# A bidirectional hybrid trunk on one core: the instruction order from a timeline simulation

## The chip, the cores and the metric

The kernel runs on one of the eight cores of a Trainium2 chip. The metric is device time in microseconds (us) from the program's start to its end; lower is better. A core has five engines, each with a queue of its own that is worked off in order: TensorE (PE; its weight loads are listed as PEld), VectorE (DVE), ScalarE (ACT), GpSimd (POOL) and SyncE (SP, which here only issues DMAs). An instruction that waits for another engine holds up all that stand behind it in its queue, so the order of each queue is part of the program.

## The reference

One inference step over 384 tokens (128 of a prompt, 256 of a latent sample), width 1024, two layers. A conditioning vector gives shift, scale and gate of every sub-layer (`mod`).

```python
mod = silu(cond) @ w_mod[l] + b_mod[l]          # 6 * 1024 values per layer
shift1, scale1, gate1, shift2, scale2, gate2 = jnp.split(mod, 6, axis=-1)
m, st = mix_fn(rmsnorm(x, g[0]) * (1 + scale1) + shift1)
x = x + gate1 * rmsnorm(m, g[1])
f = jnp.square(jax.nn.relu((rmsnorm(x, g[2]) * (1 + scale2) + shift2) @ w_up)) @ w_down
x = x + gate2 * rmsnorm(f, g[3])
```

In layer 0 the mixer has an SSD (Mamba-2) and an RWKV-7 head group, in layer 1 a GLA and an mLSTM group, all of them in both directions:

```python
# RWKV-7, per head and token
s = s * exp(lw_t) - (s @ kk_t) * (kk_t * a_t) + v_t * k_t
# mLSTM, per head and token
h = num / jnp.maximum(jnp.abs(den), jnp.exp(-m_t))
```

## The kernel before

**Dense products.** Each projection is made of `dps` products on TensorE: activations and weights are split into a high and a low part, and three products are added (high by high, low by high, high by low). A weight panel `raw` is loaded by SP (line 689), its high part `wH` copied by ACT (L277), its low part `wL` taken by DVE (L235). These products wait for little and can stand almost anywhere.

**Layer 0 mixer (AB).** The recurrence of RWKV is worked in 16 steps (8 pairs of heads, 2 directions). In each a triangular matrix is inverted by five doublings. One doubling is the product `pz`, two copies `Zb` on ACT, the products `pw` and `pt`, and two subtractions on DVE that give the next `W` and `T`:

```python
pz = pairs("pz", self.AOb[n % 2], Tm)
for h in halves:
    self.acopy(Zb[h, :, h], zv[h])
pw = pairs("pw2", Zb, W)
self.tt(f(W2), f(W), pw, ALU.subtract)
self.tt(f(T2), f(Tm), pt[:, :T], ALU.subtract)
```

The products `pe`, then `pc`, end an inversion and feed the chain `pr`, `pu`, `pd`, `py` over four segments. The tiles of the inversion exist once, so the 16 inversions run one after the other. Beside them stand the SSD core (`aux`), the dense products of the input projection and of the output projection (its last panel is `wlast`), and the modulations of later sub-layers.

**Modulations.** For each of eight slices k of the conditioning, four products write four column quarters of one accumulator. The weights come from a pool of 20 tiles:

```python
for g, w in enumerate(raw.pop(0)):
    self.mm(a[32 * g:32 * g + 32], self.cond[:, k, :], w, start=k == 0, stop=k == KD - 1)
```

In the MLP of layer 0 the generator of this block is advanced once and then behind three panels of the down projection (`if j in (2, 4, 6): next(mod)`), and the rest is left for the turn to the layer 1 mixer.

**Layer 1 mixer (CD).** Four heads of GLA and four of mLSTM, with dense products between. An mLSTM head ends with the products `ps<-mv,mE` and `ps<-CN,mq`, the sum `num` and its normalisation on DVE (`den`, `mo`), a norm over the head (`hsq` on ACT, `hss` on DVE), and six transposes `ps<-const_base,mo` on TensorE. A GLA head ends with the same transposes of `go`.

**What sets the order.** The program is written as generators that are interleaved by step counts and a table of paces (`run`, line 1578). From this text a list scheduler makes each engine's queue: it keeps a simulated time for each engine, and of the instructions that are ready at that time it takes the first one in program order. What is ready when, and so the order, follows from the durations that its simulation gives. The choice of buffers in the pools follows too.

## Time and profile before

| | us |
|---|---|
| median of 3 runs | 1856.34 (1852.14 to 1859.11) |
| the profiled execution | 1855.77 |
| its span, first to last instruction | 1853.7 |
| TensorE busy in the span | 1763.3 |
| granted TensorE clock, mean | 0.98 |

The stages in the profile: opening 0 to 125 us, AB 125 to 790, output projection and the turn to the MLP 790 to 870, the MLP of layer 0 to 1145, the turn to CD to 1200, CD to 1545, the turn to 1600, the MLP of layer 1 to the end. In the views a line such as L221 is a line of the kernel, a name such as `dps<-sH,wH` is the tile written and the tiles read. TensorE's float32 products of a `mod` appear as two records each.

### The profile page before, as it was taken

Reading aid. Unit: us, or ns where it says so; the run is one execution under the profiler, and the core shown is the slowest. Engines: PE = TensorE matmul, PEld = TensorE weight load, DVE = VectorE, ACT = ScalarE, POOL = GpSimd, SP = SyncE. Lnnn points to the kernel's source line nnn. Section 1 sums busy time; section 2 is a strip of 40 time slices with the busy share of each in tenths; the row PEclk is TensorE's granted clock in tenths of the full one; section 3 lists DMA queues with packets and bytes.
Section 4 is the critical chain, followed back from the end, with each engine's and each line's share of the span. In section 5 each row is a group of like instructions: output and inputs, shape, how many; then the busy total and the mean of one; then the engine's idle time right before and its main releaser. Section 6 shows DMA issues by size and latency. Waiting matters only on the chain.

```text
span 1853.7 us, 37402 instructions
## 1 busy us (share of the span) xinstructions
PE 1763.3 (95%) x13667; PEld 1479.4 (80%) x13667; DVE 1302.7 (70%) x2992; ACT 1068.7 (58%) x2688; POOL 216.8 (12%) x270
## 2 busy tenths in 40 slices
PE   7879999999999999999999999899999998999998
PEld 3677767666666777786999997889989897999887
DVE  3698788777877888768765335686786958766434
ACT  3567475747564776646654332676676756755322
POOL 3222111120112011111000000020211212000000
PEclk9889999999999999999999999999999998999999
DMA  8332443333334322345445544333333233344432
GB/s 280 114 87 75 122 136 87 106 93 112 100 103 125 99 60 86 100 129 161 126 125 176 164 143 107 84 98 103 101 94 92 74 109 106 115 125 126 149 135 80
DMA packets 314107, 213.55 MB, mean 115 GB/s; under 512 B 39648, under 2 KB 297494, under 8 KB 313924
## 3 DMA queue, kind: packets, MB, share of 16 engines
q1 hardware_dynamic: 308756, 208.35, 38.5%
q10 hardware_dynamic: 4816, 2.69, 0.5%
q8 instruction: 107, 1.75, 0.4%
q14 instruction: 76, 0.62, 0.1%
q0 software_dynamic: 352, 0.13, 0.0%
HBM read 201.32 MB, written 9.78 MB: 114 GB/s over the span
## 4 chain that ended last, share of the span: by engine, by line
PE 76%; DVE 10%; ACT 8%; issue 3%; DMA 2%; POOL 1%; SPq 1%; DVEq 0%; ACTq 0%; POOLq 0%
PE dps L221 46%; PE o L221 7%; PE ps L221 5%; PE mod L221 3%; PE aux L221 2%; DVE wL L235 2%; PE psc L221 2%; PE py L221 1%; PE pt L221 1%; PE pr L221 1%; DVE cacc L242 1%; ACT wH L277 1%; ACT Zb L277 1%; PE pw L221 1%; PE ms L221 1%
## 5 line engine op out<-in xcount | busy, mean ns | idle before, releaser
L277 ACT ACTIVATE wH<-raw 128x256 fp32r<-128x256 f32 (+1 forms) x790 | 363.2, 480 | 430.1 <-PE dps L221 305.3
L235 DVE TENSOR_TENSOR wL<-raw,wH 128x256 fp32r<-128x256 f32 (+2 forms) x771 | 399.5, 537 | 246.3 <-ACT wH L277 242.8
L277 ACT ACTIVATE Zb<-pz 64x384 f16<-64x384 f32 x160 | 77.2, 482 | 36.2 <-PE pz L221 33.8
L242 DVE SCALAR_TENSOR_TENSOR cacc<-rows,params,cacc 128x384 f32<-128x384 f32 (+1 forms) x192 | 94.2, 491 | 0.7
L221 PE MATMUL dps<-sH,wH 128*128 128x384 f32 x232 | 85.3, 369 | 5.5 <-DVE m L235 4.9
L221 PE MATMUL dps<-sL,wH 128*128 128x384 f32 x232 | 80.0, 345 | 0.3 <-DVE sL L235 0.2
L221 PE MATMUL dps<-sH,wL 128*128 128x384 f32 x232 | 79.4, 343 | 0.5 <-DVE wL L235 0.5
L221 PE MATMUL dps<-h0H,wH 128*128 128x384 f32 (+1 forms) x147 | 59.5, 406 | 11.9 <-ACT h0H L277 7.3
L235 DVE TENSOR_TENSOR AO<-AHb,rwmask 128x768 f16<-128x768 f16 (+1 forms) x112 | 60.0, 537 | 7.4 <-PE pz L221 5.7
L235 POOL TENSOR_TENSOR BK<-BK,kkk 128x768 f32<-128x768 f32 x16 | 33.8, 2110 | 222.3 <-DVE BK L239 151.3
L221 PE MATMUL mod<-xT,cond 128*32 128x384 f32 (+1 forms) x320 | 56.2, 490 | 3.7 <-DVE Q L235 2.5
L221 PE MATMUL dps<-h6H,wH 128*128 128x384 f32 (+2 forms) x147 | 54.8, 373 | 2.7 <-ACT wH L277 2.7
L221 PE MATMUL dps<-h4H,wH 128*128 128x384 f32 (+1 forms) x147 | 54.4, 375 | 2.1 <-ACT h4H L245 2.1
L221 PE MATMUL dps<-h2H,wH 128*128 128x384 f32 (+1 forms) x147 | 54.8, 374 | 0.0
L235 POOL TENSOR_TENSOR gDb<-gb 128x384 f32<-128x384 f32 x28 | 33.2, 1187 | 172.4 <-DVE gb L2224 73.2
L221 PE MATMUL dps<-h6H,wL 128*128 128x384 f32 (+2 forms) x147 | 50.8, 346 | 1.4 <-DVE wL L235 1.4
L221 PE MATMUL dps<-h0H,wL 128*128 128x384 f32 (+1 forms) x147 | 51.9, 353 | 0.0
L221 PE MATMUL dps<-h1H,wH 128*128 128x384 f32 (+1 forms) x147 | 51.8, 352 | 0.0
L221 PEld LDWEIGHTS dps<-sH,wH 128*128 128x128 f32 x232 | 43.6, 189 | 10.1 <-issue 5.6
L221 PE MATMUL dps<-h0L,wH 128*128 128x384 f32 (+1 forms) x147 | 51.5, 356 | 0.0
L221 PE MATMUL dps<-h1H,wL 128*128 128x384 f32 (+1 forms) x147 | 51.0, 347 | 0.0
L221 PE MATMUL dps<-h1L,wH 128*128 128x384 f32 (+1 forms) x147 | 51.0, 353 | 0.0
(1163 smaller groups left out, 5455.1 us busy)
## 6 DMA issues: line engine op xcount, KB each, us to landing
raw<-in_w_mlp_up SPq DMA_DIRECT2D x64, 512.0 KB
raw<-in_w_mlp_down SPq DMA_DIRECT2D x64, 512.0 KB
raw<-in_w_in_ab SPq DMA_DIRECT2D x204, 128.0 KB
xT<-in_w_mod SPq DMA_DIRECT2D x128, 192.0 KB
raw<-in_w_in_cd SPq DMA_DIRECT2D x192, 128.0 KB
raw<-in_w_mod SPq DMA_DIRECT2D x64, 192.0 KB
raw<-in_w_mod SPq DMA_DIRECT2D x32, 256.0 KB
raw<-in_w_out_cd SPq DMA_DIRECT2D x64, 128.0 KB
```

The lines of the kernel that those rows point to most:

```text
L221: self.nc.tensor.matmul(out, lhsT, rhs, start=start, stop=stop)
L235: (eng or self.nc.vector).tensor_tensor(out=out, in0=a, in1=b, op=op)
L242: self.nc.vector.scalar_tensor_tensor(out=out, in0=a, scalar=s, in1=b, op0=op0, op1=op1)
L277: self.nc.scalar.activation(out=out, in_=in_, func=AF.Copy)
```

## The change

The scheduler's simulation of durations is switched from its default to the timeline simulation, for the whole program:

```diff
-    with tile.TileContext(nc) as tc:
+    with tile.TileContext(nc, schedule_with_timeline_sim=True) as tc:
         build(tc, I, O)
```

The instructions, their engines and their operands stay the same; the order in each queue and the buffers change. Three places on TensorE's queue follow, each first of before, then of the change.

The MLP of layer 0, TensorE, at the modulations of layer 1 (`mod`), among the down projection (`dps<-f...`). Before:

```order
L221 MATMUL dps<-f31H,wH 128x384
L221 MATMUL dps<-f31L,wH 128x384
L221 MATMUL dps<-f31H,wL 128x384
L221 MATMUL mod<-raw,cond 32x384 x4
L221 MATMUL dps<-f0H,wH 128x384
L221 MATMUL dps<-f0L,wH 128x384
```

The change:

```order
L221 MATMUL dps<-f15H,wL 128x384
L221 MATMUL dps<-f16H,wH 128x384
L221 MATMUL dps<-f16L,wH 128x384
L221 MATMUL mod<-raw,cond 32x384
L221 MATMUL dps<-f16H,wL 128x384
L221 MATMUL dps<-f17H,wH 128x384
L221 MATMUL dps<-f17L,wH 128x384
```

Before, the 32 products stand in three groups of four in this MLP and twenty at the turn to CD; in the change 21 stand alone, two blocks have six and two, all among the down projection, and three stand at the turn.

CD, TensorE, the end of the last mLSTM head (`mo`). Before, with 54 `dps` rows between the last `ps<-CN,mq` and this piece:

```order
L221 MATMUL dps<-sH,wH 128x384
L221 MATMUL dps<-sL,wH 128x384
L221 MATMUL dps<-sH,wL 128x384
L232 MATMUL ps<-const_base,mo 128x128 x3
L221 MATMUL dps<-sH,wH 128x384
L221 MATMUL dps<-sL,wH 128x384
L221 MATMUL dps<-sH,wL 128x384
```

The change:

```order
L221 MATMUL dps<-sH,wL 128x384
L221 MATMUL ps<-mv,mE 128x257 x3
L221 MATMUL ps<-CN,mq 128x257
L221 MATMUL ps<-mv,mE 128x257
L221 MATMUL ps<-CN,mq 128x257
L232 MATMUL ps<-const_base,mo 128x128 x6
L221 MATMUL dps<-sH,wH 128x384 x2
```

The six transposes moved up to stand right behind the products that their input comes from.

AB, TensorE, the same doubling of the twelfth inversion (from its last `pz` to its first `pw`). Before:

```order
L221 MATMUL pz<-T,AO_793 128x64
L221 MATMUL pu<-R,WF 64x64 x2
L221 MATMUL dps<-h2H,wH 128x384
L221 MATMUL dps<-h2L,wH 128x384
L221 MATMUL dps<-h2H,wL 128x384
L221 MATMUL dps<-h3H,wH 128x384
L221 MATMUL dps<-h3L,wH 128x384
L221 MATMUL dps<-h3H,wL 128x384
L232 MATMUL aux<-const_base,X 128x128
L232 MATMUL aux<-const_base,Y 128x128
L221 LDWEIGHTS Zb
L221 MATMUL pw_10449<-W,Zb 128x64
```

The change:

```order
L221 MATMUL pz<-T,AO_793 128x64
L221 MATMUL pu<-R,WF 64x64 x2
L221 MATMUL py<-Q,UV 64x64
L221 LDWEIGHTS Zb
L221 MATMUL pw_10449<-W,Zb 128x64
```

The dense products that stood between have moved to earlier steps. Over the steps the number of `dps` products is, before and in the change: before the first `pe` 356 and 403; then 30, 94, 92, 52, 72, 96, 68, 52, 72, 96, 68, 60, 44, 140, 61 and 125, 120, 96, 66, 75, 123, 0, 72, 120, 60, 3, 0, 129, 36, 170; in the last step, up to the first `dps<-sH,wlast`, 155 and 10.

## Rows read from the trace of the kernel before

**Rows 1.** The page: busy times, and the chain that ended last, by line.

```profile
PE 1763.3 (95%) x13667; PEld 1479.4 (80%) x13667; DVE 1302.7 (70%) x2992; ACT 1068.7 (58%) x2688; POOL 216.8 (12%) x270
...
PE dps L221 46%; PE o L221 7%; PE ps L221 5%; PE mod L221 3%; PE aux L221 2%; DVE wL L235 2%; PE psc L221 2%; PE py L221 1%; PE pt L221 1%; PE pr L221 1%; DVE cacc L242 1%; ACT wH L277 1%; ACT Zb L277 1%; PE pw L221 1%; PE ms L221 1%
```

**Rows 2.** Windows by stage: busy time and records of each engine.

```profile
core 0: us, PE busy (x) PEld busy (x) DVE busy (x) ACT busy (x) POOL busy (x), PEclk, DMA share, GB/s
...
125.00:790.00 665.00, 641.36 (x7212) 466.55 (x7212) 541.78 (x1344) 421.09 (x1071) 98.27 (x105) 0.99 0.35 100
...
870.00:1145.00 275.00, 273.30 (x1562) 269.64 (x1561) 147.84 (x290) 126.83 (x266) 7.92 (x14) 1.00 0.47 139
1145.00:1200.00 55.00, 45.81 (x272) 37.16 (x271) 39.55 (x101) 29.91 (x78) 1.53 (x8) 0.94 0.32 76
1200.00:1545.00 345.00, 332.89 (x2047) 312.85 (x2047) 263.76 (x601) 242.76 (x706) 51.06 (x66) 0.99 0.36 100
```

**Rows 3.** The chain that ended last, in the first MLP: start, us, what.

```profile
1093.63 33.48 PE dps L221 x192
```

**Rows 4.** TensorE's timeline there: start, duration, line, operation, records.

```profile
1092.51 0.33 PE L221 MATMUL dps<-f31H,wL 128*128 128x384 f32 x1
1092.77 0.85 PE L221 MATMUL mod<-raw,cond 128*32 128x384 f32 x8
1093.56 0.44 PE L221 MATMUL dps<-f0H,wH 128*128 128x384 f32 x1
1093.83 0.34 PE L221 MATMUL dps<-f0L,wH 128*128 128x384 f32 x1
```

**Rows 5.** TensorE's timeline in AB, a single `mod` product.

```profile
198.59 0.83 PE L221 MATMUL mod<-xT,cond 128*32 128x384 f32 x2
199.35 0.45 PE L221 MATMUL dps<-h3H,wL 128*128 128x384 f32 x1
```

**Rows 6.** TensorE's timeline at the turn to CD; in brackets idle time, and what ended it.

```profile
1148.85 3.43 PE L221 MATMUL mod<-raw,cond 128*32 128x384 f32 x40
...
1152.22 3.49 PE L221 MATMUL warm<-nh,const_base 128*128 128x384 f32 x10
...
1163.32 0.58 PE L221 MATMUL dps<-h0H,wH 128*64 128x384 f32 x1 [7.33 <-ACT h0H L277]
```

**Rows 7.** TensorE's waits in CD: total, times, longest.

```profile
PE ps L232 <- DVE mo L239: 6.3, 3, 2.9
```

**Rows 8.** TensorE's timeline at the end of the last mLSTM head.

```profile
1530.01 0.60 PE L221 MATMUL ps<-CN,mq 128*128 128x257 f32 x2
...
1539.80 0.49 PE L232 MATMUL ps<-const_base,mo 128*128 128x128 f32 x3
```

**Rows 9.** Windows behind the wait of rows 6.

```profile
1163.30:1167.00 3.70, 3.68 (x12) 3.50 (x13) 3.14 (x6) 3.64 (x9) 0.00 (x0) 0.50 0.00 0
1167.00:1171.00 4.00, 4.00 (x24) 3.62 (x23) 3.44 (x9) 4.00 (x12) 0.52 (x2) 1.00 0.00 0
```

**Rows 10.** Windows of inversion steps 5, 11, 12, and the last stretch of AB.

```profile
360.50:424.10 63.60, 60.46 (x613) 42.58 (x612) 48.94 (x117) 30.76 (x89) 12.18 (x12) 0.95 0.33 95
...
645.30:680.60 35.30, 34.90 (x459) 26.95 (x458) 31.99 (x83) 23.16 (x58) 7.74 (x7) 1.00 0.25 64
680.60:712.90 32.30, 30.70 (x378) 22.61 (x378) 27.14 (x65) 28.63 (x71) 2.69 (x3) 1.00 0.20 58
...
799.80:844.40 44.60, 42.58 (x336) 34.11 (x335) 25.40 (x68) 18.63 (x48) 2.08 (x3) 1.00 0.53 161
```

**Rows 11.** TensorE's timeline in step 12: start, first doubling, and the shortest one.

```profile
680.62 0.34 PE L221 MATMUL pe<-T,i128h 128*128 128x384 f16 x1
...
690.68 0.35 PE L221 MATMUL pz<-T,AO 128*128 128x64 f16 x6
...
706.57 0.34 PE L221 MATMUL pz<-T,AO 128*128 128x64 f16 x6
707.99 0.35 PE L221 MATMUL pw<-W,Zb 128*128 128x64 f16 x6 [0.41 <-ACT Zb L277]
708.27 0.38 PE L221 MATMUL pt<-Zb,W 64*64 64x64 f16 x12
709.62 0.35 PE L221 MATMUL pz<-T,AO 128*128 128x64 f16 x6
```

## The prediction

> **What bounds the kernel now.** I read the page first: TensorE is busy for 95% of the span, and the products `dps` alone are 46% of the chain that ended last [rows 1]. A busy TensorE need not be at its peak, so the second view is the table of windows by stage [rows 2]. Compare the first two columns of each row. The MLP has 273.30 us of work in 275, the layer 1 mixer (CD) 332.89 in 345, and the layer 0 mixer (AB) 641.36 in 665. No other engine comes near its window. So TensorE's queue is the bound nearly everywhere, and a new order can act in two ways only: it changes what a row costs by what stands next to it, or it puts a row so early that TensorE stands and waits, with everything behind it in the queue. An order can win back at most the idle time: 23.6 us in AB, 12.1 in CD, 9.2 at the turn from MLP to CD.
>
> **The change, part by part.** No instruction is added or removed, so each term is a price times a count of places in the order of TensorE.
>
> *MLP of layer 0, modulations.* In a row of dense products one comes every 33.48/192 = 0.174 us [rows 3]. A group of four `mod` products (eight records, two a product) follows a `dps` after 0.26 us, the next `dps` comes 0.79 later, and the one after that 0.27 later [rows 4]. That is 0.97 us over the dense spacing (0.26 + 0.79 + 0.27 − 2 × 0.174). A single `mod` product (two records) holds TensorE for 0.76 us [rows 5], as long as four: the four write different column quarters of one accumulator and overlap, one alone has nothing to overlap with. The order of before has three groups of four in this MLP; after has 21 singles and eight products in two blocks (six and two, three groups at this price), so 24 groups. The 21 more cost 21 × 0.97 = **+20.4 us**, on an engine with 1.7 us of idle time in that stage. Were packing worth nothing, the same 20 products more would cost about 20 × 0.17 = 3 us: I take the first, since it is the measured row.
>
> [...]
>
> *Turn from MLP to CD.* Before, the other 20 `mod` products stand here (3.4 us), then the warming products; yet TensorE still waits 7.33 us for `h0H` [rows 6]. They were hidden, so taking them out gives nothing back. Three remain, now ahead of the `ms` products that the residual's `rr` needs, one group plus its two changes: **+1.0**.
>
> *CD, ends of the mLSTM heads.* Here the transposes `ps<-const_base,mo` need the chain num, den, mo, hsq, hss, mo on DVE and ACT. In the last head the last `ps<-CN,mq` is at 1530.01 and the transposes at 1539.80 [rows 8], 9.8 us apart, with 54 products between, and no wait. In the three heads ahead of it TensorE did wait, 6.3 us in sum [rows 7]. In the order of after, followed by buffer number, work of over 13 us still stands between in heads 1 and 2, but about 1.4 us in head 3 and nothing in head 4. So TensorE waits 9.8 − 1.4 = 8.4 and 9.6 us there, and keeps about 2.5 us of the old waits in heads 1 and 2: 8.4 + 9.6 + 2.5 − 6.3 = **+14.2**. Bounds: +6 (a chain that runs in 6 us when DVE and ACT have less beside it) and +20 (the 13 us that the earlier heads needed).
>
> [...] Lost: about 1.8 us, twice: **+3.6**. [...]
>
> *AB.* The 16 inversions run one after another; between the first rows of two of them (a "step") stands whatever dense work the scheduler puts there. Counting steps from 0 at 157.4 us, in before the counts of `dps` vary from 30 to 140; in after from 0 (steps 6 and 11) to 170, and the last stretch before `dps<-sH,wlast` keeps 10 of its 155. Four terms:
> – The last stretch takes 44.6 us [rows 10]. Its 145 products cost 145 × 0.174 = 25.2 us in their new places. What is left is serial: four rounds of `pr`, `pu`, `pd`, 12 hops at about the 1.4 us of a bare hop [rows 11], 2 us ahead and an estimated 8 behind, 27 us. So it shrinks by 17.6, not 25.2: +7.6.
> – Changes of tile size: 945 before, 869 after by the order, at some 0.09 us each (0.26 against 0.174): −7.
> – Step 11 (35.3 us) loses 60 products and 8 `aux`, 10.4 and about 2 us (an estimate), and would be 22.9. An inversion can't be so short: 10.06 us from its `pe` to the next first `pz`, and five doublings of at least 3.05 [rows 11], 25.3. +2.4.
> – Steps 6, 10 and 11 have 0, 3 and 0 products to stand in the hops of 15 doublings. In before six (1.04 us) often stood between `pz` and `pw`; now a few small `pu` and `py` do. Each doubling has two bare hops, together 2.77 us. I take 0.4 us lost per doubling, nearer to nothing because step 12 ran such hops with TensorE busy 30.70 us of 32.30 [rows 10]: +6.
> Sum **+9**. Bounds: −23 (the moved products fill AB's 23.6 us of idle time, no hop is lost, tile changes count) and +45 (all hops of the 15 doublings bare, 41).
>
> Opening and second MLP: nothing; independent products change places there. Sum: 20.4 + 1.0 + 14.2 + 3.6 + 9 = 48.2 on the profiled run's 1855.8 us, which is the median of the runs (1856.3) within 0.6. **1904 us.**
>
> **Rivals.**
> *Faster.* AB has no idle time left: the moved products fill its 23.6 us, the tile changes give 7, the last stretch is all gain, 17.6. 1855.8 − 48.2 + 20.4 + 1.0 + 14.2 + 3.6 = 1847, and below that if the mo chain is short (+6): 1839. For it: fewer tile changes, and the serial tail carried dense work it did not need. Against: 23.6 us is many small waits and changes, of which the order keeps most. It decides if AB gives more than 48 us, or 40 with the short chain. Chance 0.07.
> *No difference.* The mo chain is short (+6) and AB gives 21 to 40 us, by the same means in part: 1866 to 1847. Chance 0.12.
> *Every uncovered hop is lost.* AB +45, mo +20: 1855.8 + 45 + 20 + 25 = 1946. For it: the queue is in order, and the light steps have nothing else. Against: step 12. Chance 0.10.
> *Clock.* [...] Chance 0.08. [...]
> *The forecast*, 1880 to 1930: 0.63.
>
> **How the numbers follow.** The forecast's sum is the time. The range leaves out the faster case, half of no difference and the far end of the lost hops: 1862 to 1942. What can be told from no change is 0.5% (1847 to 1866). Faster 0.07; same 0.12; slower 0.81.
>
> **What would show it.** In the changed kernel's trace: `mod` singles in the first MLP at 0.76 us each, and that stage 20 us longer; two waits of 8 to 10 us of TensorE for `mo` at the end of CD, with granted clock under 1 behind them; a last AB stretch near 27 us; light steps near 25 to 33 us. Wrong if the MLP does not grow (products not on the path), if `mo` is ready in half the time, or if AB as a whole moves by more than 25 us either way.

## The result, and the profile after

The change makes the kernel slower: 1983.49 us (median; 1975.4 to 1988.98) against 1856.74 in the same job, a ratio of 1.067 (1.0644 to 1.0697). The forecast was 1904, its range 1862 to 1942: the direction was right, the size was not, and the time lies outside the range. The page of the changed kernel, as in [rows 1]:

```profile
PE 1830.2 (92%) x13667; PEld 1538.2 (78%) x13667; DVE 1320.1 (67%) x2992; ACT 1072.5 (54%) x2688; POOL 218.5 (11%) x270
...
PE 51%; DVE 4%; ACT 2%; issue 1%; DMA 0%; DVEq 0%; ACTq 0%
PE dps L221 36%; PE o L221 7%; PE ps L221 4%; PE mod L221 1%; DVE m L235 1%; DVE acc L235 1%; DVE wL L235 1%; PE ms L221 0%; PE ps L232 0%; PE py L221 0%; DVE xT L235 0%; ACT nh L245 0%; ACT sH L277 0%; DMA raw<-in_w_mod 0%; PE pm L221 0%
```

The instructions are the same, yet TensorE is busy for 66.9 us longer than in [rows 1], so the same records take up more of its time, and there are 59.5 us more in which it stands (span 1980.1 against 1853.7). Where it happens is read from windows cut at the same instructions in both traces: the first and the last `pe`, the first `dps<-sH,wlast`, and the `warm` products at the two turns behind it. First the windows of before, then those of the change (columns as in [rows 2]):

```profile
157.40:799.80 642.40, 622.30 (x7052) 451.42 (x7052) 523.13 (x1306) 405.25 (x1034) 90.57 (x97) 0.99 0.36 102
...
844.40:1152.20 307.80, 305.44 (x1734) 287.41 (x1734) 173.96 (x341) 145.05 (x309) 14.66 (x20) 0.99 0.47 139
1152.20:1574.20 422.00, 393.14 (x2360) 364.39 (x2357) 324.91 (x731) 287.99 (x819) 65.07 (x85) 0.97 0.35 96
```

```profile
177.20:904.30 727.10, 674.13 (x7140) 512.03 (x7138) 539.60 (x1321) 408.18 (x1033) 93.09 (x98) 0.91 0.32 91
723.20:760.20 37.00, 33.34 (x369) 24.10 (x369) 20.44 (x50) 16.02 (x36) 1.82 (x1) 0.55 0.01 2
904.30:936.10 31.80, 27.04 (x214) 13.18 (x210) 13.00 (x36) 7.84 (x19) 0.00 (x0) 0.79 0.71 232
936.10:1263.60 327.50, 321.13 (x1702) 290.54 (x1701) 170.39 (x329) 143.37 (x302) 14.98 (x24) 0.98 0.41 119
1263.60:1699.30 435.70, 394.39 (x2359) 366.63 (x2358) 329.49 (x739) 288.89 (x824) 62.92 (x81) 0.96 0.35 95
```

| stretch | before | after | difference | forecast |
|---|---|---|---|---|
| to the first `pe` | 157.4 | 177.2 | +19.8 | +8.2 (47 `dps` moved in) |
| 15 steps, first to last `pe` | 642.4 | 727.1 | +84.7 | +18.4 (98 `dps` moved in, the three small terms) |
| last stretch of AB | 44.6 | 31.8 | −12.8 | −17.6 |
| output projection, MLP, turn to CD | 307.8 | 327.5 | +19.7 | +20.4 and part of +1.0 |
| CD and the turn behind it | 422.0 | 435.7 | +13.7 | +17.8 |
| second MLP | 279.5 | 280.8 | +1.3 | 0 |

Two thirds of the loss stand in the second row. Its window tells of two things at once: the time in which TensorE stands grew from 20.1 to 53.0 us, and its busy time by 51.8, of which the 98 moved products account for 17 and leave some 35; the granted clock fell from 0.99 to 0.91. Step 11 (counted from 0; 723.2 to 760.2, the second row of the change) shows it at its worst, at a clock of 0.55; the steps of [rows 10] have 0.95 to 1.00.

In the MLP TensorE's timeline shows what the forecast's first term describes, a single `mod` that holds the engine for 0.76 us [rows 5]:

```profile
1147.35 0.33 PE L221 MATMUL dps<-f8L,wH 128*128 128x384 f32 x1
1147.61 0.83 PE L221 MATMUL mod<-raw,cond 128*32 128x384 f32 x2
1148.37 0.44 PE L221 MATMUL dps<-f8H,wL 128*128 128x384 f32 x1
```

In CD the waits, as in [rows 7], and the end of the last mLSTM head, as in [rows 8]:

```profile
PE dps L221 <- ACT h0H L277: 9.8, 1, 9.8
PE ps L232 <- DVE mo L239: 8.8, 2, 6.8
PE ms L221 <- DVE acc L235: 3.9, 1, 3.9
PE ps L221 <- DVE mE L235: 3.3, 2, 2.0
PE mn L232 <- DMA mnr<-in_state_mlstm_n: 2.6, 1, 2.6
```

```profile
1659.01 0.62 PE L221 MATMUL ps<-CN,mq 128*128 128x257 f32 x2
1666.48 1.54 PE L232 MATMUL ps<-const_base,mo 128*128 128x128 f32 x6 [6.84 <-DVE mo L239]
```

The wait for `mo` grew from 6.3 to 8.8 only. In the whole stretch TensorE stands 12.4 us longer (41.3 against 28.9) and is busy only 1.3 longer: the rest of CD's loss is spread over the other waits.

Now the doublings. A hop is the way from `pz` to `pw` (through `Zb` on ScalarE) or from `pt` to the next `pz` (through `T` on VectorE); it is bare when no `dps` stands in it. TensorE's timeline of the change has here an overfull hop (step 5), then the middle of step 11:

```profile
474.36 0.34 PE L221 MATMUL pz<-T,AO 128*128 128x64 f16 x6
474.53 0.89 PE L221 MATMUL pn<-t,const_base 128*128 128x384 f32 x2
475.26 0.38 PE L221 MATMUL aux<-C,B 128*128 128x128 f32 x2
475.57 0.33 PE L221 MATMUL pr<-S,KR 64*64 64x64 f32 x4
475.84 0.44 PE L221 MATMUL dps<-h0H,wH 128*128 128x384 f32 x1
...
479.24 0.34 PE L221 MATMUL dps<-h6L,wH 128*128 128x384 f32 x1
479.51 0.33 PE L221 MATMUL pu<-R,WF 64*64 64x64 f32 x4
479.77 0.35 PE L221 MATMUL pw<-W,Zb 128*128 128x64 f16 x6
```

```profile
746.67 0.33 PE L221 MATMUL pz<-T,AO 128*128 128x64 f16 x6 [0.24 <-DVE T L235]
747.28 0.33 PE L221 MATMUL pu<-R,WF 64*64 64x64 f32 x4 [0.27 <-DVE R L235]
748.40 0.40 PE L221 MATMUL py<-Q,UV 128*64 128x64 f32 x2 [0.79 <-DVE UV L239]
748.73 0.50 PE L221 MATMUL pw<-W,Zb 128*128 128x64 f16 x6
749.16 0.53 PE L221 MATMUL pt<-Zb,W 64*64 64x64 f16 x12
```

ScalarE's timeline has the two copies for the first of them:

```profile
475.64 0.98 ACT L277 ACTIVATE Zb<-pz 64x384 f16<-64x384 f32 x2
```

`Zb` is there at 476.6, and the `pw` that the inversion waits for stands behind 20 `dps` until 479.77. In step 11 no `dps` stands there, only small products that wait themselves (0.27 us for `R`, 0.79 for `UV`), and what TensorE then does is slow (`pw` in 0.50 us, `pt` x12 in 0.53, against 0.35 and 0.38 in [rows 11]).

### The profile page after: what moved, and what is told of

Its sections match the earlier page's. It is cut to its first block, busy times and chain, and to the rows that moved or that the text cites. A ratio compares the mean times of both kernels' runs of the same rounds, so it can differ in the third digit from the quotient of the medians.

```text
span 1980.1 us, 37540 instructions
## 1 busy us (share of the span) xinstructions
PE 1830.2 (92%) x13667; PEld 1538.2 (78%) x13667; DVE 1320.1 (67%) x2992; ACT 1072.5 (54%) x2688; POOL 218.5 (11%) x270
## 4 chain that ended last, share of the span: by engine, by line
PE 51%; DVE 4%; ACT 2%; issue 1%; DMA 0%; DVEq 0%; ACTq 0%
PE dps L221 36%; PE o L221 7%; PE ps L221 4%; PE mod L221 1%; DVE m L235 1%; DVE acc L235 1%; DVE wL L235 1%; PE ms L221 0%; PE ps L232 0%; PE py L221 0%; DVE xT L235 0%; ACT nh L245 0%; ACT sH L277 0%; DMA raw<-in_w_mod 0%; PE pm L221 0%
## 5 line engine op out<-in xcount | busy, mean ns | idle before, releaser
L235 DVE TENSOR_TENSOR wL<-raw,wH 128x256 fp32r<-128x256 f32 (+2 forms) x771 | 394.2, 532 | 304.9 <-ACT wH L277 294.3
L242 DVE SCALAR_TENSOR_TENSOR cacc<-rows,params,cacc 128x192 f32<-128x192 f32 (+1 forms) x192 | 97.8, 513 | 1.4
L221 PE MATMUL mod<-xT,cond 128*32 128x384 f32 (+1 forms) x320 | 59.5, 505 | 4.0 <-DMA xT<-in_w_mod 2.9
L221 PEld LDWEIGHTS dps<-h0H,wH 128*128 128x128 f32 x147 | 28.8, 197 | 42.6 <-ACT h0H L277 14.3
L221 PE MATMUL psc<-KR,BK 64*128 64x128 f32 x384 | 52.9, 327 | 7.4 <-DVE BK L235 4.5
L221 PEld LDWEIGHTS psc<-KR,BK 64*128 64x128 f32 x384 | 42.4, 219 | 13.1 <-DVE BK L235 5.3
L221 PE MATMUL dps<-h0L,wH 128*128 128x384 f32 (+1 forms) x147 | 51.8, 359 | 0.0
L221 PE MATMUL dps<-h4H,wH 128*128 128x384 f32 (+1 forms) x147 | 50.2, 350 | 1.4 <-ACT h4H L245 1.4
L221 PE MATMUL dps<-h5H,wH 128*128 128x384 f32 (+1 forms) x147 | 50.7, 345 | 0.0
L221 PE MATMUL dps<-h4L,wH 128*128 128x384 f32 (+1 forms) x147 | 50.6, 349 | 0.0
```

Source lines behind the costliest of these rows:

```text
L221: self.nc.tensor.matmul(out, lhsT, rhs, start=start, stop=stop)
L235: (eng or self.nc.vector).tensor_tensor(out=out, in0=a, in1=b, op=op)
L242: self.nc.vector.scalar_tensor_tensor(out=out, in0=a, scalar=s, in1=b, op0=op0, op1=op1)
```

## The experiments

**How a queue is held.** Most kernels below build the program twice. The first build gives the order of each queue; in the second, chosen queues are chained in that order, and the scheduler makes the others with the simulation of that build:

```diff
+    first, _ = _program(inputs, False)
+    queue = {}
...
+                queue.setdefault(str(x.engine).rsplit(".", 1)[-1], []).append(x.name)
...
+        for engine in PIN_ENGINES:
+            prev = None
+            for name in queue[engine]:
...
+                if prev is not None:
+                    tc.add_manual_dep(x, prev, info, reason="pin")
+                prev = name
...
+    nc, arrays = _program(inputs, True, pin)
```

(False is the default simulation, True the timeline simulation.) Each ratio is to the kernel before in the same job.

**1 to 3. TensorE's queue of before**, in the opening and AB, from the first MLP on, and everywhere.

```diff
+PIN_ENGINES = ('PE',)
+PIN_STAGES = ('setup', 'ab')
```

> Timeline simulation for the whole program, but TensorE's queue in the opening and in the layer 0 mixer (AB) is held to the order of before; the other engines' queues and all later stages are scheduled as in the change. Theory A (the new order of TensorE's queue in AB is what costs 92 us there): AB ends near 844 to 855 us, the total near 1983 - 92 = 1891, between 1885 and 1905. Rival B (the new queues of DVE, ACT and SP in AB are late, and TensorE only shows it): AB still ends near 936 and the total stays near 1980. In between by as much as each has a share.

> The converse: TensorE's queue as in before from the first MLP to the end, the opening and AB left to the timeline simulation. Theory A, with the prediction's terms for the first MLP (+20) and the layer 1 mixer (+14): 1983 - 34 = 1949, AB still ending near 936 us. Rival B: about 1980, since the single modulations and the early transposes would not be what these two stages lost.

> TensorE's queue as in before in the whole program, the other queues and the choice of buffers from the timeline simulation. Theory A: the whole loss is in TensorE's order, so 1850 to 1865. Rival B: 1930 or more, as late DVE, ACT and SP instructions still hold TensorE up.

Measured: run 1 1993.05 us, a ratio of 1.0714 (1.0697 to 1.0731); run 2 1973.46, 1.0615 (1.0591 to 1.0639); run 3 1979.16, 1.0633 (1.0604 to 1.0662). With TensorE's old order AB is no faster: the other queues, made anew around it, cost as much. In runs 2 and 3 the output projection, the MLP and its turn are back at 309.9 and 312.5 us (327.5 in the change), CD is not (438.0 and 438.1).

**4. The mirror**: TensorE's queue of the change, the others made by the default simulation.

```diff
+    first, _ = _program(inputs, True)
+    nc, arrays = _program(inputs, False, pin)
```

> The default simulation, with TensorE's queue held to the order of the change in the whole program; the other engines are scheduled by the default simulation around it. Theory A: 1970 to 1995, as slow as the change. Rival B: 1856 to 1900, since the queues that would be at fault are those of before.

Measured: 2088.85, 1.1244 (1.1207 to 1.128): the slowest of all, and above what either theory gave.

**5 to 8. More queues of before**: ScalarE, VectorE, both, or SP and POOL beside TensorE.

```diff
+PIN_ENGINES = ('PE', 'Activation', 'DVE')
```

> Timeline simulation with the queues of TensorE and ACT held to the order of before in the whole program; DVE, SP and POOL free. The last runs showed that TensorE's order alone gives nothing back (1979 us with it, 1983 without). Theory B1 (ACT's queue is late: in that run TensorE waits for UV, Zb and fo of ACT): 1880 to 1910. Theory B2 (DVE's queue is late: it waits for R, T and BK of DVE): 1950 to 1985. Both queues, each in part: 1910 to 1950.

> The same with TensorE and DVE held, and ACT, SP and POOL free. Theory B2: 1870 to 1910. Theory B1: 1950 to 1985.

> TensorE, ACT and DVE held to the order of before, SP (the loads) and POOL free. B1 and B2 alike: 1855 to 1875, since the three queues that work on each product are those of before. Theory C (the loads or POOL come at other times): still above 1920.

> TensorE, SP and POOL held to the order of before, ACT and DVE free. B1 and B2: 1960 to 1985, nothing is won by SP and POOL. Theory C: 1855 to 1890.

Measured: run 5 1965.03, 1.0555 (1.0527 to 1.0583); run 6 1919.91, 1.0308 (1.0247 to 1.037); run 7 1864.8, 1.002 (1.0002 to 1.0037); run 8 1978.69, 1.0627 (1.0598 to 1.0656). With three queues held the loss is gone but for some 4 us; what run 7 leaves free (SP, POOL, the choice of buffers) holds next to nothing beside them, and run 8 gains nothing from SP and POOL. What ScalarE's queue is worth depends on VectorE's: 14 us without it, 55 with it. The windows of the third run (TensorE alone held) and of the seventh (all three held), steps of AB and CD:

```profile
173.20:903.30 730.10, 664.74 (x7053) 481.89 (x7052) 532.94 (x1308) 411.76 (x1035) 88.47 (x97) 0.92 0.32 90
...
1261.20:1699.30 438.10, 397.28 (x2360) 370.30 (x2357) 327.59 (x732) 290.96 (x816) 64.03 (x85) 0.95 0.35 93
```

```profile
158.50:808.00 649.50, 627.05 (x7053) 452.87 (x7052) 524.22 (x1307) 405.19 (x1034) 89.99 (x97) 0.98 0.36 101
...
1157.80:1581.30 423.50, 395.92 (x2359) 367.71 (x2356) 324.61 (x730) 288.20 (x818) 64.69 (x85) 0.96 0.36 96
```

TensorE runs the same 7053 records in the same order in both. Late partners cost it 80.6 us, 42.9 as standing (65.4 against 22.5) and 37.7 as longer busy time at a lower clock (0.92 against 0.98). An estimate from the two rows, with the 1.00 and 0.50 that the windows of [rows 9] show: a mean of 0.92 over 730.1 us is some 117 us at 0.50, 0.98 over 649.5 some 26. At 0.50 `dps` start 0.32 us apart (the change, 1669.88 to 1672.76), against 0.174 [rows 3], so about half of the difference is lost: 45 us, near the 37.7. Other runs with this order on TensorE bear it out: the busy time of the steps is 621.5 us at a clock of 0.99 (run 15), 647.5 at 0.94 (run 12) and 663.1 at 0.92 (run 5).

In CD too: the `mo` transposes stand in their old place in both, and TensorE waits for them 16.2 us in the one and 5.5 in the other. First the third run, then the seventh:

```profile
PE ps L232 <- DVE mo L239: 16.2, 3, 7.6
```

```profile
PE ps L232 <- DVE mo L239: 5.5, 3, 2.2
```

**9. All three, in the opening and AB alone. 10. ScalarE and VectorE of before, TensorE free.**

```diff
+PIN_ENGINES = ('PE', 'Activation', 'DVE')
+PIN_STAGES = ('setup', 'ab')
```

```diff
+PIN_ENGINES = ('Activation', 'DVE')
```

> The queues of TensorE, VectorE and ScalarE stand as before in the opening and the layer 0 mixer (AB) alone; from the first MLP on everything stands as in the change. Theory D (the loss has two separate places: +92 in the opening and AB from the queues of VectorE and ScalarE, and the modulations and the layer 1 mixer behind it): AB ends near 853, the MLP with its turn takes some 327, the layer 1 mixer 436 to 438, and the kernel 1890 to 1900. Rival (the order of VectorE and ScalarE hurts everywhere, and AB only shows it first): the MLP and the layer 1 mixer get longer than in the change, above 1910. Rival (the gain in AB is lost again behind it, since transfers were late with it): above 1930.

> The queues of ScalarE and VectorE stand as before in the whole program, TensorE's is free and made by the timeline simulation. Theory D (TensorE's order in AB costs nothing by itself, the other two queues carry the loss): 1860 to 1885, with the modulations among the down projection at some +17 to +20 if they are placed there again. Rival (TensorE's order is harmful once its partners are on time, which the runs with it held could not show): 1900 or above.

Measured: run 9 1895.08, 1.0181 (1.0152 to 1.021), and run 10 2068.6, 1.1116 (1.1081 to 1.1152). Run 9 is as theory D has it. Run 10 is not: TensorE's queue, made anew around two old ones, costs 204 us against the seventh run. In its AB steps TensorE is busy for 709.69 us, at a clock of 0.87, and waits where the doublings are:

```profile
166.20:955.90 789.70, 709.69 (x7062) 532.86 (x7061) 520.69 (x1306) 403.77 (x1033) 95.34 (x97) 0.87 0.29 83
```

```profile
PE pw L221 <- ACT Zb L277: 16.0, 17, 2.2
PE pz L221 <- DVE T L235: 12.2, 17, 1.9
```

So the first reading of runs 1 to 8, that TensorE's order is harmless and the other two carry the loss, falls: the three queues are worth something as a set only.

**11, 12, 15. Part of VectorE's queue.** TensorE and ScalarE as before; on VectorE the inversion and its chain, with the preparation of the next step, with the panels' `wL`, and with both.

```diff
+DVE_OF = ('rw_inverse', 'rw_chain', 'rw_prep', 'rw_tokmajor', 'rw_shared', 'rw_bonus', 'rw_low', 'rw_tail')
...
+                if engine == "DVE" and of.get(n) not in DVE_OF:
+                    continue
```

> TensorE and ScalarE as before; of VectorE's queue only the instructions of the RWKV inversion, its chain, and the preparation of the next step (BK, KR, EBL and what leads to them) stand in their old order among themselves; the low halves of the weight panels (wL) and the rest are free. With nothing of VectorE held it was 1965, with all of it 1865. Theory P (the preparation of the next step is what stands in front of the inversion and the chain): most of the 100 us come back, 1865 to 1900. Theory L (it is the weight panels): 1935 to 1965. Both in equal parts: near 1915.

> TensorE and ScalarE as before; of VectorE's queue only the instructions of the RWKV inversion, its chain and the low halves of the weight panels (wL) stand in their old order among themselves; the preparation of the next step and the rest are free. Theory P: 1935 to 1965, near the run with nothing of VectorE held. Theory L: 1865 to 1900. Both in equal parts: near 1915.

> TensorE and ScalarE as before; of VectorE's queue the inversion, the chain, the preparation of the next step and the low halves of the weight panels stand in their old order among themselves, the rest is free. Held alone beside the chain, the preparation gave 55 us and the panels 22 of the 100. If they add up: 1885 to 1895, and the last 20 us lie in the rest of VectorE's queue. Rival (each only makes room for the other, one of them is enough): 1905 to 1912. Rival (they are worth more together, since what stood in front of the chain was now the one and now the other): 1865 to 1880.

Measured: run 11 1910.53, 1.0268 (1.0231 to 1.0305); run 12 1943.56, 1.0444 (1.0413 to 1.0475); run 15 1898.1, 1.0197 (1.0163 to 1.0232). Of the 100 us between runs 5 and 7, run 11 gives 55, run 12 gives 22, and run 15 with both parts 67, less than the sum. The inversion and its chain are held in all three and in no run alone, so the 55 and the 22 may count the same thing twice. The other 33 lie in the rest of VectorE's queue, but not in the steps of AB, as run 15 has them:

```profile
173.20:821.50 648.30, 621.46 (x7052) 452.38 (x7050) 527.12 (x1307) 406.40 (x1034) 91.09 (x97) 0.99 0.36 101
```

They take 719.0 us in run 5, 648.3 here, and 649.5 in run 7: beside the old queues of TensorE and ScalarE, the chain, the preparation and the panels are all of VectorE's queue that the steps need. Of the 33, some 15 stand in the opening (173.2 against 158.5) and 11 in CD (434.8 against 423.5).

**13. The same part of VectorE's queue, TensorE and ScalarE free.**

```diff
+PIN_ENGINES = ('DVE',)
```

> Of VectorE's queue the RWKV inversion, its chain and the preparation of the next step stand in their old order among themselves; TensorE, ScalarE and the rest of VectorE are free, as in the change. Theory P (in the change itself the preparation that stands in front of the inversion and the chain makes the loss): AB shrinks by 40 to 55 us, 1925 to 1945. Rival M (the queues cost what they cost as a set; the old place of the preparation helps only where TensorE and ScalarE stand as before too): 1970 or slower, up to the 2070 of the run with two queues held.

Measured: 2025.37, 1.0883 (1.0856 to 1.091), slower than the change. The old place of the chain and the preparation is worth 55 us beside the old queues and costs 42 beside new ones. It is no cause by itself.

**14. All three queues up to the end of the first MLP.**

```diff
+PIN_STAGES = ('setup', 'ab', 'mlp0')
```

> TensorE, VectorE and ScalarE as before in the opening, AB and the first MLP; the layer 1 mixer and the second MLP as in the change. With the opening and AB alone it was 1895, with the whole program 1865. If the predicted price of the modulations (+20 in the first MLP) is right and additive: 1875 to 1880, the first MLP with its turn near 306 us and the layer 1 mixer near 437. Rival (the single modulations only hide elsewhere, their price comes back at the turn or behind it): 1888 to 1897.

Measured: 1875.72, 1.0088 (1.0058 to 1.0119), 19.4 us below run 9. The stretch from `wlast` to the turn to CD, in run 9 and here:

```profile
850.50:1173.90 323.40, 320.06 (x1732) 287.33 (x1733) 170.84 (x330) 143.07 (x302) 15.50 (x24) 1.00 0.44 131
```

```profile
853.40:1159.00 305.60, 303.95 (x1735) 286.71 (x1735) 174.16 (x341) 145.31 (x309) 14.71 (x20) 1.00 0.48 140
```

That is 17.8 us, nearly all of it busy time at a clock of 1.00, as a price of the products would be. CD, scheduled as in the change in both, is shorter here too (430.4 us against 437.8, where about 437 stood), so the 19.4 of the medians are not the MLP's alone. From here to run 7 are another 11 us, 7 of them in CD (423.5 there).

**16, 17. No waits between products and panel copies**, in the queues of the change and in those of before, all five held. In AB the dense products with 128-column panels read one kept panel in place of fresh ones, which leaves that part of the computation out. (The kept panel takes the room of two `wL` tiles.)

```diff
+        one = cfg.get("one") and (nk, ncol) == (2, 128)
+        tag, bufs = ("w", cfg["split"]) if not one or "kept" in cfg else ("kept", 1)
...
+        if one:
+            return cfg.setdefault("kept", (h, lo))
         return h, lo
```

> The queues stand exactly as in the change. In AB the dense products with 128-column panels read one panel that is split once and kept, in place of the fresh one (this part of the computation is left out); all copies wH and subtractions wL are still made, at full size, in their places in the queues, but no product reads them, so no copy waits for a product to free its tile and no product waits for a copy. Theory W (in the change's own set, VectorE and ScalarE stand at panel copies that wait for TensorE's products, 113 waits of wH and 71 of wL in AB, and the chain stands behind them): AB shrinks by 40 us or more, 1915 to 1940, while the same edit in the queues of before gains 10 at most. Rival C (the waits lie between the inversion, its chain and the preparation themselves; the panels only fill time in which their engines would stand anyway): within 15 us of the change, 1965 to 1985.

> The same edit in the queues of before (one kept panel read in AB, the copies made but not read; this part of the computation is left out). Theory W: 1848 to 1862, since TensorE is busy for 97% of AB there. Rival C: the same; it is the control of the run beside it, and what counts is whether the distance between the two stays near 125 us or falls below 85.

Measured: run 16 1989.02, 1.0704 (1.0686 to 1.0722), and run 17 1858.87, 1.0011 (0.9982 to 1.0041). ScalarE's longest waits in the AB steps, of the change, then of run 16:

```profile
ACT wH L277 <- PE dps L221: 92.5, 113, 3.4
ACT Zb L277 <- PE pz L221: 51.0, 37, 4.5
```

```profile
ACT Zb L277 <- PE pz L221: 75.7, 39, 5.0
ACT UV L245 <- DVE UV L239: 39.5, 27, 4.6
```

The 113 waits of the panel copies are gone, ScalarE waits for `pz` instead, and the 15 steps take 730.7 us (727.1 in the change). Theory W falls: these waits only fill time in which ScalarE would stand for TensorE anyway.

**18. Dense products bunched, on TensorE alone.** Run 17 with 245 rows of TensorE's queue moved: in 23 pairs of doublings the `dps` between the first `pw` and the next one go ahead of the first, into its hop from `pz`. No other queue is touched.

```diff
+    queue["PE"] = lumped(queue["PE"])
...
+    for (a, b), (c, d) in zip(hops, hops[1:]):
+        rows = [n for n in q[b:d] if kind(n) == "dps"]
...
+        if ok:
+            ahead[b] = rows
```

> The queues of before with the one kept panel (the run of 1859 is its control; the same part of the computation is left out). One thing more: in 23 pairs of hops of the inversion, the dense products between the first pz's answer and the second's (245 rows of TensorE's queue) are moved ahead into the first hop, their own order kept. Of the 80 hops from pz to pw 29 then have no dense product (12 in before, 37 in the change) and 14 have 16 or more (0 and 21); of the 79 hops from pt to pz 33 have none (11 and 31). The queues of VectorE and ScalarE are untouched. Theory H (in the change's own set TensorE's queue bunches the dense products, so that most hops stand bare while others are overfull): 39 of the change's 45 more bare hops, so up to 39/45 of the 85 us that the steps lost, 1890 to 1935. Rival N (it does not matter in which hop of a step a dense product stands; what costs is the order on VectorE and ScalarE): 1850 to 1870.

Measured: 1891.78, 1.0178 (1.0144 to 1.0213), 32.9 us over run 17. The steps of AB in run 17 and here:

```profile
155.00:804.60 649.60, 628.74 (x7053) 456.72 (x7052) 525.07 (x1307) 401.78 (x1034) 90.46 (x97) 0.97 0.36 101
```

```profile
157.60:827.70 670.10, 629.62 (x7052) 464.70 (x7052) 524.26 (x1306) 402.77 (x1034) 91.32 (x97) 0.96 0.35 98
```

The same products in other hops, and TensorE stands for 40.5 us in place of 20.9. The hops themselves, with `dps` counted in the queues and times taken from the starts on the timeline (from the last `pz` to the first `pw` or `pt`: 80 hops; from the last `pt` to the next `pz`: 79, of which 15 lead from one inversion to the next):

| | before | change | run 17 | run 18 |
|---|---|---|---|---|
| `pz` to `pw`: hops with no `dps` / 16 or more | 12 / 0 | 37 / 21 | 12 / 0 | 29 / 14 |
| their time, us | 157 | 250 | 158 | 199 |
| `pt` to `pz`: hops with no `dps` / 16 or more | 11 / 12 | 31 / 25 | 11 / 12 | 33 / 12 |
| their time, us | 446 | 457 | 451 | 433 |

Rival N falls. Theory H holds for direction and place, at the low end of its range: the steps of the profiled executions lose 20.5 us where the change lost 84.7, the medians 32.9 where AB with its opening lost 91.7. So bunching on TensorE alone makes a quarter to a third, nearly all of it as standing; the clock hardly moved (0.97 to 0.96).

## Why the prediction was right, and where it was wrong

**What bounds the kernel.** Right for before. It was wrong to conclude that an order can act only by what stands next to a row or by a row that is too early on TensorE: in the change the clock of the AB steps fell too (0.91 against 0.99), and the other engines' queues decide when TensorE's rows may start (80.6 us between runs 3 and 7, with one order on TensorE).

**MLP, modulations, +20.4.** Right: +19.7 with the output projection and the turn in the change, 17.8 in that stretch between runs 9 and 14, and 15 to 18 given back in runs 2 and 3. The price of a single product held (0.76 us). Packing was not worth nothing; the turn's +1.0 can't be told apart from it.

**CD, +14.2 and +3.6 for the clock behind it.** Near in size (+13.7 of 17.8) by luck, wrong in its mechanism. I had two waits of 8.4 and 9.6 us for `mo`, from a chain of 9.8 us. That was the distance of two rows with 54 products between them and no wait, so no more than an upper bound of the chain; it took 7.5 us in the last head (1659.01 to 1666.48). The third head's wait for `mo` is 1.9, with 2.0 for `mE` just ahead of it, and heads 1 and 2 have none, so the waits for `mo` grew by 2.5 only. No run shows the 3.6 for the clock behind two such waits: behind the one of 6.84 us ten `dps` start 0.32 us apart at a clock of 0.50 (1669.88 to 1672.76), some 1.3 us more than at the 0.174 of [rows 3], and the whole stretch is busy 1.3 us longer. Run 3 has the transposes in their old place, and CD stays at 438.1; run 7 brings it back to 423.5 with VectorE and ScalarE. So putting the transposes back is not enough; no run moved them alone.

**AB, +9: the step that failed.** Measured +91.7, far beyond the 25 us that I had named as a sign of being wrong. Its parts:
– Last stretch: −12.8 where −17.6 stood. It took 31.8 us, and the clock there was 0.79.
– "Steps 6, 10 and 11 have 0, 3 and 0 products to stand in the hops of 15 doublings": I counted dense products by step, and a hop is covered or not by what stands in that hop. Of 159 hops 68 stand bare in the change, 23 before; 21 of the 80 to a `pw` hold 16 to 24 products, and the `pw` stands behind them. I had 30 bare hops (15 doublings). Run 18 prices the bunching at 20 to 33 us.
– "0.4 us lost per doubling, nearer to nothing because step 12 ran such hops with TensorE busy 30.70 us of 32.30": step 12 of before has 44 dense products and a clock of 1.00. Step 11, forecast at 25.3 us, took 37.0, at 0.55; steps 6 and 10 took 39.2 and 40.7, where 25 to 33 stood.
– Opening, 0 beside the moved products: +19.8 with 8.2 of them. Run 9 gives it back (159.1).
– No term at all for the new order on VectorE and ScalarE. Beside TensorE's old order, late partners cost the steps 80.6 us (run 3 against run 7), 37.7 of it as longer busy time at a lower clock.

**The rivals.** "Every uncovered hop is lost" (1946) and "Clock" (chance 0.08) stood apart, as if the one did not come with the other. They came together: in step 11 TensorE has no dense product, waits in its hops, and has a granted clock of 0.55 in the mean. Bare hops alone hardly brought the clock down: run 18 has 62 of them (68 in the change), spread over steps that keep their dense products, and its clock is 0.96 (0.97 in run 17). "Faster" and "No difference" found nothing.

**What the runs leave open.** Shown: the loss is in the queues of TensorE, VectorE and ScalarE, as a set (run 7 against 1 to 6, 8, 10, 13); with the same TensorE queue, late partners cost about as much in longer busy time at a lower clock as in waits (37.7 and 42.9 us, run 3 against 7); bunching on TensorE alone costs 33 us, 20.5 of them in the steps (run 18); waits for panel copies are not it (run 16). Not settled: how the other 60 us or more of AB divide, in the change's own queues, between the orders on VectorE and ScalarE, the small products in the hops, and the clock, which no run held up by itself. No run held VectorE's whole queue, or ScalarE's, alone. That the timeline simulation bunches because its durations differ from the chip's is likely, but it was only argued.

## What to carry to other kernels

When a list scheduler's durations change, the queues of all engines change together; read them hop by hop along the serial chain, and count what stands in each hop, not in each step. Don't hold one queue to find a culprit and believe the answer: here holding one or two good queues gave anything from half of the loss back (run 6) to 85 us more of it (run 10), and only all three told. Where a chain of short hops and dense filler share an engine, an even filling (mostly six products to a hop from `pz` to `pw`, before) is worth keeping: undoing it on TensorE alone cost 33 us.

## What was not expected of the hardware

TensorE's granted clock was 0.55 in the mean of a step (step 11) in which it was busy 33.34 us of 37.00 (90%). Windows of 4 us in the change, the first at the end of the step before, where the clock fell, the last in the step behind:

```profile
708.00:712.00 4.00, 3.05 (x41) 2.29 (x40) 3.77 (x7) 2.25 (x7) 1.27 (x1) 0.87 0.17 48
...
728.00:732.00 4.00, 4.00 (x54) 3.53 (x55) 1.90 (x5) 2.28 (x6) 0.98 (x1) 0.50 0.00 0
...
740.00:744.00 4.00, 4.00 (x39) 2.62 (x34) 1.98 (x6) 0.82 (x3) 0.00 (x0) 0.50 0.00 0
...
772.00:776.00 4.00, 2.29 (x39) 1.87 (x40) 2.70 (x7) 2.17 (x5) 1.43 (x1) 0.98 0.35 107
```

A granted clock of 0.50 stands beside a TensorE that is busy throughout, mostly with small products and with no `dps`, and 0.98 beside one that is busy for 2.29 us of 4. What brought it down was not shown: in the steps of AB the change, with 53.0 us in which TensorE stands, has 0.91, and before, with 20.1, has 0.99, but run 18, with 40.5, has 0.96. Of step 11 the busy column alone would not have told it.
